# Two filler tiles that shift every SBUF buffer of the left side by 160 bytes

## The chip, the cores and the metric

The kernel runs on one core of one Trainium2 chip. The metric is the device time of one execution in microseconds (us), told as the median of several runs. Before the change it is 2169.11 us, the median of 3 runs between 2166.14 and 2170.45 us.

## The reference

Two post-norm layers over 512 tokens of width 2048, all in float32:

```python
# layer 0: one projection feeds stick-breaking attention (8 heads x 128) and a pooling mixer
h = x @ w_in                                   # 2048 x 6144
q, k, v, g_a, u, g_b = split(h)
o_a = stick_breaking_attention(q, k, v)
o_b = multiscale_pool(u, w_pool, pool_scale)   # windows 2, 4, 8, 16
y = concat([o_a * silu(g_a), o_b * silu(g_b)]) @ w_out
x = layer_norm(alpha * x + y)
# layer 1: RWKV-7 time mixing, 32 heads x 64
xr, xw, xk, xv, xa, xg = token_shift_mixes(x, mu)
r, k, v, g = xr @ w_r, xk @ w_k, xv @ w_v, xg @ w_g      # four 2048 x 2048 products
w, a = lora(xw), lora(xa)
o = wkv7_scan(r, decay(w), k, v, kk, a)        # state of 64 x 64 a head, 512 steps
y = ((group_norm(o) + bonus) * silu(g)) @ w_o
x = layer_norm(alpha * x + y)
```

## The kernel before

Every large float32 product is made of three products of a shorter format (fp32r): both operands are split into a high part and the rest (`split`, L133: ScalarE copies the high part, VectorE or GpSimd subtracts it), and TensorE adds high x high, high x low and low x high into the same PSUM bank (`mm3`, L138 to L142; `mm3b`, L484 to L488). A matmul has a moving operand, here mostly 512 columns that stream through the array, and a stationary one of 128 columns, the weights of the array, which a separate load (PEld) brings in while the matmul before it still streams. Both are read from the SBUF.

The core goes through these stages, in the order of time (us from the start of the span):

- 0 to 611: layer 0's input projection (`gemm_a`, L156): moving operand is the transposed input `x0_k` (tile `x` in the profile), stationary are the split weights `whi` and `wlo`. Between its groups of 24 matmuls small pieces of the attention are issued (`pump`, L45, L175); the gate columns from about 380 us on have almost none.
- 611 to 800: layer 0's output projection and layer norm (`proj_ln`, L421): here the weights `whi` and `wlo` move, 512 columns (three blocks) or 256 (two), and the gated rows `mixed` are stationary; the sums are called `gb`.
- 810 to 1430: layer 1's projections for k, r and g, again `gemm_a`: moving is the shifted input `mx`, stationary `whi` and `wlo`. k and r have side jobs between the groups (`ssq`, `low`, `loa`, `prew`, `prea`, `pb`), g has none after its first column block. In the first column block of each the tiles `mx` are still being made (`mixes`).
- 1430 to 1940: the RWKV recurrence in chunks (`scan`, L812), small float32 products with waits on each other, and between them the fourth projection v (`vps`, `vproj`, L842), whose weights come from another pool, `swp`.
- 1940 to 2168: output projection of layer 1 (`y`, `gb`) and the last layer norm. `proj_ln` is called without its first column block here, which the end of the scan has done as `y`. The next block (c0 = 512) still takes its weights from `swp`, the ones after it from the pool `wp1` (L1210, `start`, L1213).

Each engine runs its instructions in program order. The order is set by the code and, in the scan, by planned slots; the change touches neither.

What the change touches is where tiles lie. The pools of the SBUF are stacked from two sides: from the left upwards (`cst`, `wp`, `x0`, `att`, `set`, `stmp`, `res1`, `wp1` and others), and from the right downwards those opened with `side="right"` (`cst1`, `mix0` with `mixed`, `mx`, `swp`, `ld`). A pool's place follows from the sizes of what was opened before it on its side. Each tile of 128 partitions takes its bytes at the same address in every partition.

The product, the weights' tiles and the loop that reads them:

```python
149        self.nc.sync.dma_start(raw, ap)
151        hi = pool.tile([P, ww], F32R, tag="whi", name="whi", **kw)[:, :a * b]...
152        lo = pool.tile([P, ww], F32R, tag="wlo", name="wlo", **kw)[:, :a * b]...
...
172                for n in range(2):
173                    self.mm3(ps[n], hi[:, kk, n * P:(n + 1) * P], lo[:, kk, n * P:(n + 1) * P],
174                             xs[k][:, 0, :], xs[k][:, 1, :], k == 0, k == kblocks - 1)
```

One block of 128 weights is 512 bytes of a partition and one moving operand is 2048, so within one stage all moving operands start at one address modulo 512 and all weights at one.

Of the kernel before, what the change touches and what calls it, by code (L numbers as in the profile page):

```python
# [8 lines left out]
F32 = mybir.dt.float32  # L9
# [8 lines left out]
P = 128  # L18
# [16 lines left out]
class Kernel:  # L35
# [17 lines left out]
    def setup(self):  # L53
        nc, tc, ctx = self.nc, self.tc, self.ctx
        self.cst = ctx.enter_context(tc.tile_pool(name="cst", bufs=1))
        self.dram = ctx.enter_context(tc.tile_pool(name="dram", bufs=1, space=DRAM))
        self.lctx = ctx.enter_context(ExitStack())
        self.open_pools()
        c = self.cst
        ident = self.ident = c.tile([P, P], F32, name="ident")  # L60
        make_identity(nc, ident)
        self.eps = {}
        for e in (LN_EPS, GN_EPS):
            t = self.eps[e] = c.tile([P, 1], F32, name=f"eps{len(self.eps)}")
            nc.gpsimd.memset(t, e)
# [1140 lines left out]
    def layer1_out(self, x1_d, mixed, y_d):  # L1206
        nc, tc, i = self.nc, self.tc, self.i
        with ExitStack() as ctx:
            rp = ctx.enter_context(tc.tile_pool(name="res1", bufs=6))
            wp = ctx.enter_context(tc.tile_pool(name="wp1", bufs=2))  # L1210
            bv = {}

            def start(c0):  # L1213

                if c0 == 1024:
                    self.wp, self.ww = wp, 1024
                    for n, ap in (("g1", i["ln_g"][1:2]), ("b1", i["ln_b"][1:2])):
                        t = bv[n] = rp.tile([P, D], F32, name="ln" + n, bufs=1)
                        nc.sync.dma_start(t, ap.to_broadcast([P, D]))

            def residual(t, c0, w):
                r = rp.tile([P, 512], F32, tag="xr", name="xr")[:, :w]
                nc.sync.dma_start(r, x1_d[t * P:(t + 1) * P, c0:c0 + w])
                return r

            def after(t, sf, mean, rstd):
                g, b = bv["g1"], bv["b1"]
                out = lambda sl: nc.sync.dma_start(self.out[0, t * P:(t + 1) * P, sl], sf[:, sl])
                rstd = rstd()
                cut = 1792 if t == NT - 1 else 1024  # L1230
                dve = [slice(c, min(c + 512, cut)) for c in range(0, cut, 512)]
                rest = [slice(c, min(c + 512, D)) for c in range(cut, D, 512)]
                for sl in dve:
                    nc.vector.scalar_tensor_tensor(sf[:, sl], sf[:, sl], mean, g[:, sl], ALU.subtract, ALU.mult)
                nmr = rp.tile([P, 1], F32, tag="nmr", name="nmr", bufs=2)
                nc.vector.scalar_tensor_tensor(nmr, mean, -1.0, rstd, ALU.mult, ALU.mult)
                for sl in rest:
                    nc.scalar.activation(sf[:, sl], sf[:, sl], AF.Identity, scale=rstd, bias=nmr)
                    nc.gpsimd.tensor_mul(sf[:, sl], sf[:, sl], g[:, sl])
                    nc.gpsimd.tensor_add(sf[:, sl], sf[:, sl], b[:, sl])  # L1240
                for sl in dve:
                    nc.vector.scalar_tensor_tensor(sf[:, sl], sf[:, sl], rstd, b[:, sl], ALU.mult, ALU.add)
                    out(sl)
                for sl in rest:
                    out(sl)
                yield

            def first(t):
                y = rp.tile([P, 512], F32, tag="y", name="y", bufs=2)
                nc.sync.dma_start(y, y_d[t])  # L1250
                return y

            self.proj_ln(ctx, i["od_w_o"][0], mixed, residual, after, first, start)
# [29 lines left out]
```

## Time and profile before

| | |
|---|---|
| median of 3 runs | 2169.11 us |
| the profiled execution | 2169.39 us, its span 2167.7 us |
| mean granted TensorE clock | 0.988 of full speed |
| PE (matmul) busy | 2107.6 us, 97% |
| PEld (weight load) busy | 1690.7 us, 78% |
| DVE / ACT / POOL busy | 1274.2 / 952.1 / 265.1 us |
| 128x512 matmuls of layer 0's input projection | 2304, mean 389 to 392 ns |
| 128x512 matmuls of layer 1's k, r and g | 2304, mean 398 to 399 ns |

A matmul's duration in these rows runs from its start until its last column has been written, and the next one starts long before that. What a stream of them costs is the distance from start to start: a stretch in which nothing else runs, divided by the count of matmuls in it.

### The profile page before, as it was taken

To read this page: it belongs to the slowest core of one execution; us is meant where nothing else is said; L and a number is where in the kernel's file an instruction comes from. 1 tells how busy PE (TensorE), PEld (TensorE's weight loads), DVE (VectorE), ACT (ScalarE), POOL (GpSimd) and SP (SyncE) were. 2 spreads that over 40 slices of the span, in tenths; PEclk is the share of its full clock that TensorE was granted. 3 is DMA by queue.
4 is the path that set the end of the run, shared out by engine and by line. 5 is a ranking of instruction groups with operands and counts; after the bars stand their busy time and mean duration, and the time that the engine had idled before them with its cause. 6 is when DMAs were issued, how large, how long until landed. Compare 5 with 4: busy or idle time off the path is not lost. (4 is left out here: it accounts for less than half of the span.)

```text
span 2167.7 us, 33268 instructions
## 1 busy us (share of the span) xinstructions
PE 2107.6 (97%) x12915; PEld 1690.7 (78%) x12915; DVE 1274.2 (59%) x2557; ACT 952.1 (44%) x1663; POOL 265.1 (12%) x333
## 2 busy tenths in 40 slices
PE   8999999999999989998999989999999999999997
PEld 7888888888887887776788768867777777767786
DVE  4334335454433368677777872276787877876336
ACT  3335445332321258455555652254555555554211
POOL 0000000000000000233000020022333333310003
PEclk9999999999999999999999999998999999999998
DMA  5322222323233453554466663321232332332633
GB/s 188 97 73 83 79 73 68 98 93 102 94 106 116 132 175 113 159 169 143 161 221 215 215 234 131 107 68 55 89 99 74 100 102 69 104 111 95 228 103 112
DMA packets 214029, 262.94 MB, mean 121 GB/s; under 512 B 15768, under 2 KB 161776, under 8 KB 213104
## 3 DMA queue, kind: packets, MB, share of 16 engines
q1 hardware_dynamic: 213872, 260.83, 37.4%
q8 instruction: 101, 1.65, 0.3%
q14 instruction: 56, 0.46, 0.1%
HBM read 214.32 MB, written 46.47 MB: 120 GB/s over the span
## 5 line engine op out<-in xcount | busy, mean ns | idle before, releaser
L136 DVE TENSOR_TENSOR wlo<-wraw,whi 128x1024 fp32r<-128x1024 f32 (+1 forms) x268 | 314.1, 1175 | 501.4 <-ACT whi L135 487.1
L135 ACT CAST whi<-wraw 128x1024 fp32r<-128x1024 f32 (+1 forms) x324 | 303.4, 938 | 651.4 <-PE ga L141 319.0
L140 PE MATMUL ga<-mx,whi 128*128 128x512 f32 x768 | 305.4, 398 | 6.0 <-ACT mx L135 6.0
L141 PE MATMUL ga<-mx,whi 128*128 128x512 f32 x768 | 306.5, 399 | 3.8 <-DVE mx L136 3.8
L142 PE MATMUL ga<-mx,wlo 128*128 128x512 f32 x768 | 305.6, 398 | 0.0
L140 PE MATMUL ga<-x,whi 128*128 128x512 f32 x768 | 300.9, 392 | 0.0
L142 PE MATMUL ga<-x,wlo 128*128 128x512 f32 x768 | 299.5, 390 | 0.5 <-DVE wlo L136 0.5
L141 PE MATMUL ga<-x,whi 128*128 128x512 f32 x768 | 299.1, 389 | 0.0
L486 PE MATMUL gb<-whi,mixed 128*128 128x512 f32 (+1 forms) x576 | 198.6, 345 | 1.6 <-DVE s L437 1.6
L488 PE MATMUL gb<-wlo,mixed 128*128 128x512 f32 (+1 forms) x576 | 197.5, 344 | 2.4 <-DVE wlo L136 2.4
L487 PE MATMUL gb<-whi,mixed 128*128 128x512 f32 (+1 forms) x576 | 198.3, 344 | 0.0
L140 PEld LDWEIGHTS ga<-mx,whi 128*128 128x128 f32 x768 | 145.5, 189 | 43.7 <-ACT mx L135 7.4
L141 PEld LDWEIGHTS ga<-mx,whi 128*128 128x128 f32 x768 | 145.4, 189 | 41.7 <-DVE mx L136 6.8
L142 PEld LDWEIGHTS ga<-mx,wlo 128*128 128x128 f32 x768 | 145.5, 189 | 35.3 <-issue 0.3
L142 PEld LDWEIGHTS ga<-x,wlo 128*128 128x128 f32 x768 | 144.2, 188 | 31.4 <-DVE wlo L136 0.9
L140 PEld LDWEIGHTS ga<-x,whi 128*128 128x128 f32 x768 | 144.3, 188 | 29.4 <-ACT whi L135 0.3
L141 PEld LDWEIGHTS ga<-x,whi 128*128 128x128 f32 x768 | 144.3, 188 | 29.1
L140 PE MATMUL vps<-mx,whi 128*128 128x512 f32 x256 | 122.0, 476 | 0.3 <-ACT vT L858 0.3
L488 PEld LDWEIGHTS gb<-wlo,mixed 128*128 128x128 f32 x576 | 108.2, 188 | 17.6 <-DVE wlo L136 3.2
L486 PEld LDWEIGHTS gb<-whi,mixed 128*128 128x128 f32 x576 | 108.2, 188 | 17.4 <-DVE s L437 2.9
L487 PEld LDWEIGHTS gb<-whi,mixed 128*128 128x128 f32 x576 | 108.5, 188 | 13.7
L136 POOL TENSOR_TENSOR wlo<-wraw,whi 128x512 fp32r<-128x512 f32 x56 | 73.8, 1318 | 244.6 <-ACT whi L135 194.8
(331 smaller groups left out, 3508.1 us busy)
## 6 DMA issues: line engine op xcount, KB each, us to landing
wraw<-in_ev_w_in SPq DMA_DIRECT2D x96, 512.0 KB, 3.5
wraw<-in_ev_w_out SPq DMA_DIRECT2D x32, 512.0 KB, 3.6
wraw<-in_od_w_k SPq DMA_DIRECT2D x32, 512.0 KB, 4.5
wraw<-in_od_w_r SPq DMA_DIRECT2D x32, 512.0 KB, 4.4
wraw<-in_od_w_g SPq DMA_DIRECT2D x32, 512.0 KB, 3.5
wraw<-in_od_w_v SPq DMA_DIRECT2D x64, 256.0 KB, 2.8
ar_d<-pAR SPq DMA_DIRECT2D x16, 512.0 KB, 2.6
bk_d<-pBK SPq DMA_DIRECT2D x16, 512.0 KB, 3.3
```

Source lines behind the costliest of these rows:

```text
L135: self.nc.scalar.copy(hi, src)
L136: (eng or self.nc.vector).tensor_sub(lo, src, hi.bitcast(F32))
L140: mm(ps, ah, bh, start=start, stop=False)
L141: mm(ps, ah, bl, start=False, stop=False)
L142: mm(ps, al, bh, start=False, stop=stop)
L486: mm(ps, ah, bh, start=start, stop=False)
L487: mm(ps, al, bh, start=False, stop=False)
L488: mm(ps, ah, bl, start=False, stop=stop)
```

## The change

Two tiles are allocated that nothing reads or writes. The first, 40 x 4 = 160 bytes a partition, is the first tile of the first pool of the left side, so that every tile on the left lies 160 bytes higher. The second, 112 x 4 = 448 bytes, is the first tile of the pool `res1`, and shifts only what is allocated after it in the output of layer 1.

```diff
@@ setup
         c = self.cst
+
+        c.tile([P, 40], F32, name="pad0")
         ident = self.ident = c.tile([P, P], F32, name="ident")
@@ layer1_out
             rp = ctx.enter_context(tc.tile_pool(name="res1", bufs=6))
+            rp.tile([P, 112], F32, name="pad1", bufs=1)
             wp = ctx.enter_context(tc.tile_pool(name="wp1", bufs=2))
```

The sequence of instructions of every engine, their operands' shapes and their waits are the same in both programs; only addresses differ. The start addresses of the operands modulo 512, as the two programs allocate them:

| matmuls | count | moving, before | weights, before | moving, after | weights, after |
|---|---|---|---|---|---|
| layer 0 input, `ga<-x` | 2304 | 288 | 288 | 448 | 448 |
| layer 0 output, `gb`, 512 columns | 576 | 288 | 448 | 448 | 448 |
| layer 0 output, `gb`, 256 columns | 384 | 288 | 448 | 448 | 448 |
| layer 1 k, r, g, `ga<-mx` | 2304 | 448 | 288 | 448 | 448 |
| layer 1 v, `vps` | 768 | 448 | 448 | 448 | 448 |
| layer 1 output, `y` (by tile) | 132 / 60 | 288 / 448 | 448 | 448 | 448 |
| layer 1 output, `gb`, c0 = 512 | 192 | 448 | 448 | 448 | 448 |
| layer 1 output, `gb`, c0 = 1024 | 192 | 352 | 448 | 448 | 448 |
| layer 1 output, `gb`, 256 columns | 384 | 352 | 448 | 448 | 448 |
| scan, `xo<-M,AR` | 112 | 288 | 448 | 448 | 448 |
| scan, other products with both operands on one side | | equal shift | equal shift | | |

## Rows read from the trace of the kernel before

**Rows 1.** The page, busy time of TensorE (share of the span, instructions).
```profile
PE 2107.6 (97%) x12915; PEld 1690.7 (78%) x12915; DVE 1274.2 (59%) x2557; ACT 952.1 (44%) x1663; POOL 265.1 (12%) x333
```

**Rows 2.** The page's costliest groups: count, busy us, mean ns, idle before.
```profile
L141 PE MATMUL ga<-mx,whi 128*128 128x512 f32 x768 | 306.5, 399 | 3.8 <-DVE mx L136 3.8
...
L141 PE MATMUL ga<-x,whi 128*128 128x512 f32 x768 | 299.1, 389 | 0.0
```

**Rows 3.** PE alone by stretch: from:to, us, busy (count), granted clock, DMA share, GB/s.
```profile
535.00:600.00 65.00, 65.00 (x289) 1.00 0.31 98
1310.00:1380.00 70.00, 70.00 (x301) 1.00 0.38 121
2041.00:2059.00 18.00, 18.00 (x81) 1.00 0.75 260
2070.00:2100.00 30.00, 30.00 (x130) 1.00 0.32 104
620.00:655.00 35.00, 35.00 (x152) 1.00 0.26 90
2110.00:2150.00 40.00, 40.00 (x340) 1.00 0.29 99
```

**Rows 4.** PE groups between 2040 and 2059 us, weights from the pool swp.
```profile
L486 PE MATMUL gb<-whi,mixed 128*128 128x512 f32 x29 | 11.3, 389 | 0.0
```

**Rows 5.** PE groups between 2063 and 2100 us, weights from the pool wp1.
```profile
L486 PE MATMUL gb<-whi,mixed 128*128 128x512 f32 x52 | 20.6, 396 | 0.0
```

**Rows 6.** PE groups between 834 and 1020 us, the k stage.
```profile
L141 PE MATMUL ga<-mx,whi 128*128 128x512 f32 x224 | 88.8, 396 | 0.0
```

**Rows 7.** Tile ga between 30 and 360 us: ns min/median/max, first and last start.
```profile
L141 PE MATMUL ga<-x,whi x404: 387/389/475, 29.7 to 359.9; 128*128 128x512 f32 x135
```

**Rows 8.** PE in order of time after an interruption: start us, us, what.
```profile
521.27 0.40 PE L141 MATMUL ga<-x,whi 128*128 128x512 f32 x1
521.50 0.39 PE L142 MATMUL ga<-x,wlo 128*128 128x512 f32 x1
521.73 0.40 PE L140 MATMUL ga<-x,whi 128*128 128x512 f32 x1
521.97 0.39 PE L141 MATMUL ga<-x,whi 128*128 128x512 f32 x1
522.20 0.39 PE L142 MATMUL ga<-x,wlo 128*128 128x512 f32 x1
522.42 0.39 PE L140 MATMUL ga<-x,whi 128*128 128x512 f32 x1
```

**Rows 9.** What PE waited for between 800 and 1440 us: total us, times, longest.
```profile
PE ssq L646 <- ACT sqr L135: 6.5, 1, 6.5
PE ga L140 <- ACT mx L135: 6.0, 3, 3.9
PE ga L141 <- DVE mx L136: 3.8, 4, 1.7
```

**Rows 10.** PE groups between 613 and 748 us, output projection of layer 0.
```profile
L486 PE MATMUL gb<-whi,mixed 128*128 128x512 f32 x189 | 75.1, 397 | 1.6 <-DVE s L437 1.6
L487 PE MATMUL gb<-whi,mixed 128*128 128x512 f32 x189 | 75.0, 397 | 0.0
L488 PE MATMUL gb<-wlo,mixed 128*128 128x512 f32 x189 | 73.9, 393 | 0.0
```

**Rows 11.** PE groups by shape over the whole span: 256 columns and the scan.
```profile
L486 PE MATMUL gb<-whi,mixed 128*128 128x256 f32 x256 | 72.1, 283 | 0.0
...
L1000 PE MATMUL xo<-M,AR 128*128 128x128 f32 x224 | 49.6, 304 | 2.1 <-DVE M L1026 1.2 <-DVE M L1024 0.7
...
L487 PE MATMUL y<-wo,mixed 128*128 128x512 f32 x64 | 25.5, 399 | 0.0
...
L142 PE MATMUL po<-wh,v 128*128 128x256 f32 x8 | 2.3, 282 | 0.0
```

**Rows 12.** All engines by stretch: from:to, us, PE, PEld, DVE, ACT, POOL, clock, DMA.
```profile
400.00:600.00 200.00, 199.81 (x880) 164.57 (x879) 91.38 (x116) 62.59 (x80) 0.56 (x5) 1.00 0.31 98
800.00:1000.00 200.00, 193.31 (x835) 150.63 (x834) 140.25 (x175) 120.57 (x200) 48.02 (x47) 0.99 0.49 149
1000.00:1200.00 200.00, 193.48 (x818) 154.71 (x817) 150.19 (x211) 113.96 (x180) 13.96 (x30) 0.98 0.56 188
```

## The prediction before the run

> **What bounds the kernel now.** I read the page first, then its costliest groups, then single stretches of the matmul engine, and last the waits. PE is busy for 97% of the span [rows 1], so the question is what a matmul costs in a stream, not who waits for whom. The groups hold the first hint: the 2304 matmuls of layer 1's k, r and g (three rows like the one shown, 398 to 399 ns) last 7 to 9 ns longer than the 2304 of layer 0's input projection (389 to 392 ns) [rows 2]. Both come from the same function, with the same shape.
>
> Durations overlap, so I take the distance from start to start. In a stretch that holds nothing but one kind of matmul it is (length + 0.39 us) / count, since the count includes the matmul that is cut at the edge. Layer 0's gates: 65.39/289 = 226.3 ns. Layer 1's g: 70.40/301 = 233.9 ns. Both stretches have the full clock and no idle time [rows 3]. So 7.6 ns, 3.2%, go somewhere.
>
> Is it the address? The trace has a test of its own in the output projection of layer 1, where the same loop first takes weights from `swp` and then from `wp1`. With both operands at 448 modulo 512 it runs at 18.39/81 = 227.0 ns, and from about 2062 us on, with 352 against 448, at 30.40/130 = 233.8 ns [rows 3]; the mean duration goes from 389 to 396 ns [rows 4, 5]. Engine, line, shape and stationary tiles are the same on both sides. The fast stretch is even the one with more DMA traffic (260 against 104 GB/s), so contention with transfers doesn't explain it. In every stage I read, equal residues go with 226 to 227 ns in a steady stream and unequal ones with 233 to 234 (differences of 160 and 416), or 35.39/152 = 232.8 (difference 352, layer 0's output) [rows 3]. The fast level is seen at 288/288 and at 448/448, so it is the difference that counts, not the place.
>
> **The change part by part.** It adds, removes and moves no instruction. The filler tiles cost no time: nothing writes them. The left side moves by 160 bytes, from 288 to 448, and meets the right side's 448.
>
> *k, r and g.* 2304 matmuls go from unequal to equal: 2304 x 7.6 ns = 17.5 us. Two deductions. First, an aligned stream isn't fast at once after another job: behind an interruption the starts lie 0.23, 0.23, 0.24, 0.23 and 0.22 us apart and then settle at 0.226 [rows 8], 1.15 us for five against 5 x 0.226 = 1.13, so 20 to 25 ns lost each time. k and r have 2 x 32 groups of 24 matmuls, nearly all with a job behind them: 64 x 25 ns = 1.6 us. The misaligned stream has nothing to lose there: 396 ns in k with its side jobs [rows 6], as in g's pure stretch. That an interrupted stage still gains is seen in the attention stage, where the median is 389 ns although small jobs break in [rows 7]. Second, the first column block of each stage is fed by tiles still in the making (waits of 6.0 and 3.8 us on ACT and DVE [rows 9]); 3 x 96 matmuls can gain 2.2 us there, and I give half of it, 1.1, to longer waits. The 6.5 us wait for `sqr` stays. That leaves 17.5 - 1.6 - 1.1 = 14.8 us; bounds: 12 (the whole first blocks lost and twice the loss at the breaks) and 17.5.
>
> *Output of layer 0, 512 columns.* 576 matmuls. The three lines have 397, 397 and 393 ns against 389 when aligned [rows 10, 4]: 6.7 ns on average; from starts, 232.8 - 227.0 = 5.8 [rows 3]. I take 6.2: 3.6 us, bounds 3.3 and 3.9.
>
> *Output of layer 1, c0 = 1024.* 192 x (233.8 - 227.0) = 1.3 us.
>
> *The 256-column blocks.* 768 matmuls. The trace has no long aligned stream of 256 columns. Nearest rows: short aligned ones in the attention last 282 ns, against 283 for `gb` [rows 11], which says 0 to 1 ns; but those are all within reach of an interruption. Half of the loss of a 512-column stream would be 3.5 ns. Bounds 0 and 2.7 us; I take 1.0, nearer to the rows.
>
> *Scan and `y`.* Of the `y` matmuls 132 become equal, in bursts of three, where even aligned ones hardly reach the fast level (`y`, a mix of both, has 399 ns [rows 11]): 0.3 us. The 112 products `xo<-M,AR` (224 rows of 304 ns [rows 11]) become equal as well. `vps` was aligned before, and products with both operands on the left keep their difference. I take 0 for the scan, with 1.5 us either way: 3% of the 49.6 us of that group.
>
> *Other engines.* VectorE, ScalarE and the transfers get other addresses too. I cost this at nothing: between 400 and 1200 us PE covers them, busy for 193 to 200 of each 200 us while DVE has at most 150 and ACT 121 [rows 12].
>
> Sum: 14.8 + 3.6 + 1.3 + 1.0 + 0.3 = 21.0 us. From the profiled execution's own 2169.4 us (span 2167.7 and 1.7 around it) that makes 2148.4; the median of the runs shown is 2169.1, only 0.3 below, so the forecast is 2148 us.
>
> A rule of the Trainium skill speaks against all this: it ("TensorE: Matmul & The Clock Gate", section "Step-by-step: what each phase is for") says that TensorE has two independent read ports of the SBUF, one for the moving operand and one for the weight load, and that loading the next weights takes no bandwidth from the running matmul. By it the residue of the one against the other could not matter, and the change would give 0. The trace disagrees: 227.0 and 233.8 ns in one loop [rows 3]. The ports may be two; the rows say that what lies behind them is not indifferent to the address.
>
> **The rivals.**
>
> *Only quiet stages gain.* In k and r the side work on DVE and ACT may set the pace once PE is faster, because `prep`, the squares and the mixes share those engines with the splitting of weights. For it: DVE is busy for 140 to 150 of 200 us there, against 91 in the gates, and the waits on `mx` and `sqr` lie in these stages [rows 9, 12]. Against: outside the first column blocks PE shows no idle time in k [rows 6], and 3% less time raises DVE's share only from 0.75 to 0.77. Then k and r give nothing: 768 x 7.6 = 5.8 (g) + 3.6 + 1.3 + 1.0 = 11.7 us, so 2157.7 us.
>
> *Nothing changes.* What I took for the address is something else that differs between the stages, such as the tiles' absolute place or which pool the weights come from. For it: `swp` and `wp1` are two pools, not one pool moved. Against: two boundaries in the trace, near 611 and near 2062 us, follow the residues, with different tiles on both. Time: 2169 us. The rule on independent read ports, told above, would come to this.
>
> *Slower: the level belongs to weights at 288.* All long fast stretches of layer 0 have their weights at 288, that is 32 modulo 64, and the change takes them to 448, that is 0. Were that residue the cause, layer 0's input projection would fall to the slow level, 2304 x 7.6 = 17.5 us, and layer 1 would gain nothing: 2169.4 + 17.5 = 2187 us. It is slower from the point where layer 0's loss exceeds what of the 21 us is left. Against: the stretch from 2041 to 2059 us is fast with both operands at 448 [rows 3].
>
> **How the numbers follow.** Forecast 0.84, quiet stages alone 0.08, nothing 0.04, slower 0.04. The forecast's own range comes from its bounds: gains of 12 + 3.3 + 1.3 + 0 - 1.5 = 15 to 17.5 + 3.9 + 1.3 + 2.7 + 1.5 = 27 us, both ends unlikely together; 2143 to 2154. To hold 8 in 10 with the first rival half in, I give 2143 to 2156. A measurement of this kernel tells 0.2%, 4.3 us, from no change. Faster by more: the first two cases, 0.92. Within: 0.04. Slower: 0.04.
>
> **What would show it.** Right: the `ga<-mx` groups fall from 396 ns to about 389 in steady stretches, and their starts to 226 or 227 ns apart; `gb` in layer 0 to about 389; layer 0's input projection ends at the same time as before, near 611 us; the stage of g is shorter by some 5 us. The waits on `mx` and `sqr` stay or grow by up to 1 us. Wrong: `ga<-x` above 389 ns (the absolute place matters), `ga<-mx` at 389 with new idle time in front of it (supply bounds), or `ga<-mx` still at 396 (not the address). A scan that is longer or shorter by more than 2 us would say that the small products depend on addresses too, and break the sum.

## The result and the profile after

| | median, us | range | runs |
|---|---|---|---|
| before | 2168.39 | 2164.88 to 2170.95 | 6 |
| after | 2153.43 | 2151.27 to 2158.38 | 6 |

The ratio is 0.994, with a 95% interval from 0.9927 to 0.9953: a gain of 10 to 16 us, where 21 were forecast. The time lies inside the range, but the forecast's own 2148 lies outside the interval of the measurement; the first rival, 2157.7, is nearer: 4.3 us from the median, against 5.4.

The profiled execution of after took 2158.4 us (span 2156.7), some 5 us above its median. Single stages below are therefore shown from two traces of the same program, this one and its repetition (the first experiment), before a difference of a microsecond is believed.

First the pace, the thing the change aims at. This is PE alone by stretch in the kernel after (from:to, us, busy and count, granted clock, DMA share, GB/s):

```profile
535.00:600.00 65.00, 65.00 (x288) 1.00 0.31 98
1310.00:1380.00 70.00, 70.00 (x311) 1.00 0.38 121
620.00:655.00 35.00, 35.00 (x156) 1.00 0.27 91
2060.00:2090.00 30.00, 30.00 (x135) 1.00 0.32 103
2100.00:2140.00 40.00, 40.00 (x335) 1.00 0.29 97
```

They answer to [rows 3]. With the prediction's formula: layer 0's gates 65.39/288 = 227.0 ns (226.3 before); g 70.40/311 = 226.4 (233.9); layer 0's output 35.39/156 = 226.9 (232.8); layer 1's output at c0 = 1024 30.39/135 = 225.1 (233.8). All four 512-column streams now run at one level (one matmul more or less in the count is 1.7 ns in a window of 30 us and 0.8 ns in one of 65). The last line has 256 columns, where a matmul lasts 0.28 us: 40.28/335 = 120.2 ns against 40.28/340 = 118.5 before. That one became slower.

The page's groups and busy times say the same, and answer to [rows 1] and [rows 2] (count, busy us, mean ns, idle before):

```profile
PE 2087.6 (97%) x12915; PEld 1688.5 (78%) x12915; DVE 1272.0 (59%) x2557; ACT 951.8 (44%) x1663; POOL 266.1 (12%) x333
...
L143 PE MATMUL ga<-mx,whi 128*128 128x512 f32 x768 | 302.0, 393 | 3.8 <-DVE mx L138 3.8
...
L143 PE MATMUL ga<-x,whi 128*128 128x512 f32 x768 | 299.3, 390 | 0.0
```

`ga<-mx` fell from 399 to 393 ns, `ga<-x` stayed. PE is still busy for 97%: a share of busy time doesn't show such a gain.

But a faster stream is not yet a shorter stage. The lengths of the stages, from the start of the first matmul of one to that of the next, the last one to the end of its last matmul (us), in three traces:

| stage | before | after | after, repeated | forecast change |
|---|---|---|---|---|
| layer 0 up to its gates | 344.9 | 344.7 | 344.8 | 0 |
| layer 0's gates | 257.4 | 257.4 | 257.4 | 0 |
| layer 0's output, 512 columns | 136.6 | 132.6 | 132.7 | -3.6 |
| layer 0's output, 256 columns, and up to k | 60.1 | 62.0 | 63.3 | about -0.5 |
| k, r, g: first column blocks, together | 91.7 | 92.6 | 90.2 | -1.1 |
| k, the rest | 186.1 | 183.6 | 182.4 | k, r, g: |
| r, the rest | 183.2 | 184.0 | 183.9 | -13.7 |
| g, the rest | 159.3 | 154.5 | 154.5 | together |
| scan, from the first `vps` to the first `y` | 506.9 | 501.4 | 501.2 | 0 |
| `y` | 76.6 | 76.3 | 77.0 | -0.3 |
| layer 1's output, c0 = 512 | 46.6 | 50.3 | 47.2 | 0 |
| layer 1's output, c0 = 1024 | 45.0 | 43.5 | 43.6 | -1.3 |
| layer 1's output, 256 columns | 45.7 | 46.2 | 46.2 | about -0.5 |

Layer 0's output, g and c0 = 1024 gained what their pace says. r gained nothing, though behind its first block it has the same 672 matmuls as g, which gained 4.8 us. The scan's 5.5 us and the 50.3 come from something else (below).

What r ran into instead shows in what PE waited for between 1054 and 1238 us in the kernel after (total us, times, longest us):

```profile
PE pb L809 <- DVE rkr L138: 2.1, 4, 0.7
PE prew L144 <- DVE w2h L138: 1.3, 1, 1.3
PE pb L809 <- ACT rkr L137: 0.2, 1, 0.2
```

The same window of the kernel before has one line:

```profile
PE pb L807 <- DVE rkr L136: 0.2, 1, 0.2
```

3.4 us of new waits, on results of DVE in `prep`. DVE isn't full there, so what did it wait for itself? Its waits between 1054 and 1235 us, after:

```profile
DVE pn L792 <- DMA pk<-k_d: 28.2, 10, 5.2
DVE pn L792 <- DMA pn<-rn_d: 8.2, 3, 3.7
```

and before:

```profile
DVE pn L790 <- DMA pk<-k_d: 27.8, 10, 3.4
...
DVE pn L790 <- DMA pn<-rn_d: 5.1, 2, 3.5
```

So DVE stood still for some 33 us in r already before, in front of one product that needs a load. One of these stops in the kernel after, DVE in order of time (start us, us, what, idle before and its releaser):

```profile
1201.05 0.74 DVE L803 SCALAR_TENSOR_TENSOR pr<-pr,vec,pk 128x512 f32<-128x512 f32 x1
1201.71 1.22 DVE L138 TENSOR_TENSOR wlo<-wraw,whi 128x1024 fp32r<-128x1024 f32 x1
1202.84 0.69 DVE L138 TENSOR_TENSOR rkr<-pr,rkr 128x512 fp32r<-128x512 f32 x1
1206.80 0.75 DVE L792 SCALAR_TENSOR_TENSOR pn<-pk,hkk,pn 128x512 f32<-128x512 f32 x1 [3.27 <-DMA pk<-k_d]
1207.46 1.22 DVE L138 TENSOR_TENSOR wlo<-wraw,whi 128x1024 fp32r<-128x1024 f32 x1
```

and SP's queue around it (start us, us, what):

```profile
1201.16 0.36 SPq L801 DMA_DIRECT2D bk_d<-pBK  x1
1201.64 0.35 SPq L812 DMA_DIRECT2D bc_d<-pbc  x1
1202.09 0.81 SPq L764 DMA_DIRECT2D pk<-k_d  x1
```

The load of the next `pk` is issued at 1202.09; `pn`, which needs it, already stands at the head of DVE's queue at 1203.5. All that is behind it on DVE, splits of weights and of `rkr` among it, stands with it until 1206.8. The Trainium skill ("TensorE: Matmul & The Clock Gate", section "Step-by-step: what each phase is for") says that PE is the only engine that reorders its instructions; these rows agree: `wlo` follows `pn` without a gap, though ACT had finished its half of that split at 1203.40:

```profile
1202.36 1.04 ACT L137 CAST whi<-wraw 128x1024 fp32r<-128x1024 f32 x1
```

In the kernel before, PE's own slowness covered these stops. That is a theory from waits; the second and third experiments test it.

### The profile page after: what moved, and what is told of

It is laid out like the page before. It is cut to its first block, busy times and chain, and to the rows that moved or that the text cites. A ratio compares the mean times of both kernels' runs of the same rounds, so it can differ in the third digit from the quotient of the medians.

```text
span 2156.7 us, 33268 instructions
## 1 busy us (share of the span) xinstructions
PE 2087.6 (97%) x12915; PEld 1688.5 (78%) x12915; DVE 1272.0 (59%) x2557; ACT 951.8 (44%) x1663; POOL 266.1 (12%) x333
## 4 chain that ended last, share of the span: by engine, by line
PE 82%; DVE 9%; DMA 4%; ACT 2%; issue 1%; POOL 1%; SPq 0%; DVEq 0%; ACTq 0%
PE ga L142 14%; PE ga L144 13%; PE ga L143 13%; PE gb L488 4%; PE gb L490 4%; PE gb L489 4%; PE vps L142 4%; PE vps L143 2%; PE vps L144 2%; PE xo L1004 2%; PE sa L1010 2%; PE g L877 2%; PE xo L1002 2%; DVE wlo L138 1%; PE xo L1030 1%
## 5 line engine op out<-in xcount | busy, mean ns | idle before, releaser
L142 PE MATMUL ga<-mx,whi 128*128 128x512 f32 x768 | 301.3, 393 | 5.6 <-ACT mx L137 5.6
L143 PE MATMUL ga<-mx,whi 128*128 128x512 f32 x768 | 302.0, 393 | 3.8 <-DVE mx L138 3.8
```

The lines of the kernel that those rows point to most:

```text
L142: mm(ps, ah, bh, start=start, stop=False)
L143: mm(ps, ah, bl, start=False, stop=False)
```

## The experiments

Two questions are open. Why did r give nothing: because DVE stands still in front of `pn` (my theory), or because the load on DVE and ACT sets r's pace, whatever the order (the rival)? And does the difference between two addresses set the level of a stream (my theory), or the place of one of them (the rival)? The expectations are quoted as they were written ahead of each run.

**The change again**, the same program:

> The changed kernel once more, beside the experiments on the same chip, for a second trace. Theory A (the residue modulo 512 sets a matmul's pace, and part of the gain is lost to new waits): 2153 us within 4, ga<-mx at 227 to 228 ns from start to start, and again no gain in r behind its first column block (183 to 185 us long), because PE waits there for rkr and w2h. Rival B (what r lost was a chance of one execution): r is 177 to 179 us long in this trace.

2154.98 us (2153.70 to 2155.63), ratio 0.9938 [0.9925, 0.9951]. Its stages stand in the table above. r is again without gain; c0 = 512 is not again longer, so the 50.3 belongs to one execution: there PE waited 4.3 us for `wlo`, against 2.4 before, and ran 3.4 us at a granted clock of 0.50.

**After, with `pn` issued behind the pair's scan on DVE.** The product is the same; it is told to stand later in DVE's queue:

```diff
-        nc.vector.tensor_tensor_scan(L, ...)
+        sc = nc.vector.tensor_tensor_scan(L, ...)
...
-        nc.vector.scalar_tensor_tensor(rn, k, col(self.hv["kk"]), rn, ALU.mult, ALU.mult)
+        with self.tc.issue_after(sc.ins):
+            nc.vector.scalar_tensor_tensor(rn, k, col(self.hv["kk"]), rn, ALU.mult, ALU.mult)
```

> The changed kernel with one instruction moved: on DVE's queue the product rn = k * k_k * rn of the next pair stands behind that pair's scan, no longer ahead of the rest of the chain of the pair before it, so that DVE doesn't stand still for the load of pk. Theory A (r lost its gain because DVE, the supplier of rkr and w2h, stood still 28 + 8 us for loads at the head of its queue): these waits all but vanish, PE's waits in r (some 5 us) too, r behind its first block falls from 184 to 178 to 179 us, and the time is 4 to 6 us under the changed kernel's. Rival B (DVE's work itself is too long for a PE that is 3% faster): r stays at 183 to 185 us and the time is that of the changed kernel.

2145.11 us (2141.21 to 2149.56), ratio 0.9887 [0.9866, 0.9907]. That is 8 to 10 us under the kernel after and its repetition, where 4 to 6 were expected. In r behind its first block PE waits for nothing any more, and DVE's longest waits between 1054 and 1235 us are for ACT's half of the split and for `ptw` (total us, times, longest):

```profile
DVE wlo L138 <- ACT whi L137: 26.6, 17, 4.3
DVE pL L783 <- ACT ptw L781: 8.8, 13, 2.0
```

The lines on `pk` and `pn` are gone; DVE's stops in this window come to 36 us, against 46 in the kernel after, and they now stand ahead of what DVE is early for. r behind its first block takes 178.4 us instead of 184.0. Not foreseen: g's first block falls from 34.6 to 28.0 us as well.

**Before, with the same edit.** By my theory r has nothing to gain from it while PE is slow:

> The same move of one DVE instruction in the kernel before. Theory A: before, PE waited only 0.6 us for rkr in r, so there is at most 1 us to win: 2167 to 2169 us, r behind its first block 182 to 184 us. Rival (the standstill on DVE costs by itself, whatever the addresses): 4 to 6 us faster here as well, 2163 us.

2157.83 us (2156.19 to 2162.91), ratio 0.9957 [0.9941, 0.9973]. The expectation for r held and that for the whole missed by far: 10 us faster. The rival, that the standstill costs by itself, came nearer, though not in r. The four traces, r behind its first block and g's first block:

| us | unequal residues | equal residues |
|---|---|---|
| `pn` early: r / g's first block | 183.2 / 34.6 | 184.0 / 34.6 |
| `pn` late: r / g's first block | 182.8 / 27.3 | 178.4 / 28.0 |

r needs both edits: in these traces either alone gives next to nothing, both give 4.8 us. By the rival r could not come to 178.4 with the same work on DVE and ACT. Over all thirteen traces of this document r takes 183.2 to 186.0 us with `pn` early and `ga<-mx` at the slow pace (four traces), 181.9 to 186.5 with `pn` early and the fast pace (five), 182.8 with `pn` late and the slow pace (one) and 178.4 with `pn` late and the fast pace (three). Where the time goes is seen by column block of 96 matmuls (us, the second to the eighth of r):

| kernel | 2 | 3 | 4 | 5 | 6 | 7 | 8 |
|---|---|---|---|---|---|---|---|
| before | 25.69 | 26.17 | 26.17 | 26.17 | 26.17 | 26.17 | 26.62 |
| after | 25.05 | 25.55 | 25.55 | 25.61 | 26.09 | 26.46 | 29.64 |
| after, repeated | 25.33 | 25.55 | 25.55 | 25.55 | 25.55 | 26.03 | 30.35 |
| before, `pn` late | 25.73 | 26.17 | 26.17 | 26.17 | 26.17 | 26.17 | 26.17 |
| after, `pn` late | 25.13 | 25.55 | 25.55 | 25.55 | 25.55 | 25.55 | 25.55 |

So r did gain from the addresses, 0.6 us a block, and gave it back at its end, most of it in the last block, in which DVE also makes the first tiles `mx` for g. The slow stream doesn't always cover the stop: with the left side shifted by 32 and by 128 bytes (below; `ga<-mx` at 232 to 234 ns) PE waits 2.1 and 1.7 us for `w2h` in the last block, runs 3.4 us at a granted clock of 0.50 after that, and the block takes 29.97 and 29.77 us.

The edit did more than move `pn`: the program was ordered anew around it. From r's fourth block to the seventh the order on DVE differs by `pn` alone, and that on PE, ACT and SP not at all; what blocks 6 and 7 lost is thus shown to come from that one stop. At r's start, at the end of its last block and in g's first block other instructions of these engines change places as well, so that what is shown there is the worth of the new order, not of the one stop. g's first block needs only the second edit, in both kernels. What PE waited for there, between 1238 and 1275 us, in this experiment (in the kernel before DVE's `mx` has 3.8 us there, the whole of its line in [rows 9], and ACT's 2.2):

```profile
PE ga L141 <- DVE mx L136: 0.4, 1, 0.4
```

**Layer 0 misaligned, all else as before**, by 160 bytes ahead of x alone:

```diff
+        xp.tile([P, 40], F32, name="padx")
         xs = [...]
```

> The kernel before with a filler of 160 bytes ahead of the tiles x0 alone: layer 0's moving operands lie at 448 modulo 512, its weights stay at 288; all else is as before. Theory A (the difference counts): ga<-x goes from 227 to 234 ns from start to start and from 389 to 396 ns of duration, layer 0's input projection ends 15 to 16 us later, 2183 to 2185 us in all. Rival (weights at 288 are fast whatever moves): no change, 2168 us. Rival (two independent read ports, no effect of any address): no change as well.

2182.26 us (2181.47 to 2183.10), ratio 1.0064 [1.0049, 1.0079]: 14 us slower. PE between 545 and 610 us:

```profile
545.00:610.00 65.00, 65.00 (x279) 1.00 0.29 90
```

65.39/279 = 234.4 ns where [rows 3] have 226.3. The two stages of layer 0's input grew by 8.2 and 6.8 us. 2304 x 7.6 = 17.5 would have been the full price. A column block of 96 matmuls pays it, 0.73 us, where no job breaks in; those of the attention grew by 0.60 to 0.66 us. That fits the prediction's deduction, by which only an aligned stream loses at an interruption.

**The right side moved to meet the left, at 288:**

```diff
+        cp.tile([P, 40], F32, name="padr")
         mixed, mix_ctx = self.layer0(cp)
...
+            rp.tile([P, 112], F32, name="pad1", bufs=1)
```

> The other way to bring both sides together: the kernel before with the filler of 160 bytes on the right side, which moves that side's tiles down from 448 to 288 modulo 512, and the filler of 448 bytes in res1; the left side stays where it was. Theory A (only the difference counts): the time of the changed kernel, 2153 us within 4, with ga<-mx at 227 ns. Rival (the new place of the left side's tiles, 448, made it faster, for any engine): no change, 2168 us.

2155.05 us (2153.68 to 2161.35), ratio 0.9953 [0.9936, 0.9971]. PE in layer 0's gates and in g:

```profile
535.00:600.00 65.00, 65.00 (x289) 1.00 0.31 98
1310.00:1380.00 70.00, 70.00 (x311) 1.00 0.37 121
```

65.39/289 = 226.3 and 70.40/311 = 226.4 ns with all operands at 288, as with all at 448: the difference counts, not the place. The rival of the place is out.

**Other shifts of the left side**, by 32, 128 and 416 bytes instead of 160 and without the second filler; one time each, for the pace alone:

```diff
+        c.tile([P, 8], F32, name="pad0")      # or [P, 32], or [P, 104]
```

> The kernel before with a filler of 32 bytes on the left: weights at 320, so that moving and weights differ by 128 (k, r, g), 384 (output of layer 0) and 448 (output of layer 1, second block on). Theory A in its strict form (only equal residues are fast): 231 to 235 ns from start to start in all three, 2165 to 2171 us. Rival (any difference that is a multiple of 128 is fast, since the unit is smaller than 512): 227 ns in k, r, g, and some 2155 us.

> The kernel before with a filler of 128 bytes on the left: weights at 416, differences of 32 (k, r, g), 480 (output of layer 0) and 32 the other way (output of layer 1, second block on). Theory A in its strict form: 231 to 235 ns, 2165 to 2171 us. Rival (near is good enough, the loss grows with the distance): between 227 and 230 ns and some 2157 us.

> The kernel before with a filler of 416 bytes on the left: weights at 192, differences of 256 (k, r, g; output of layer 0) and 192 (output of layer 1, second block on). Theory A in its strict form: 231 to 235 ns, 2165 to 2171 us. Rival (the unit is 256 bytes): 227 ns in k, r, g and in layer 0's output, some 2154 us. Rival (half of 512 is the worst place): above 236 ns and over 2172 us.

2161.28, 2167.67 and 2157.69 us, beside 2166.84 for the kernel before; the first and the third lie between the times expected by theory and rival. PE between 1310 and 1380 us, by 32:

```profile
1310.00:1380.00 70.00, 70.00 (x303) 1.00 0.37 121
```

by 128:

```profile
1310.00:1380.00 70.00, 70.00 (x301) 1.00 0.35 113
```

by 416:

```profile
1310.00:1380.00 70.00, 70.00 (x310) 1.00 0.37 118
```

That is 70.40/303 = 232.3, 233.9 and 227.1 ns, at differences of 128, 32 and 256 bytes between moving operand and weights. 256 is as good as 0: "modulo 512" in the change's description, and in my prediction, is twice too strict.

**The second experiment with a second filler of 128 bytes**, which should suit 256 columns and hurt 512:

```diff
-            rp.tile([P, 112], F32, name="pad1", bufs=1)
+            rp.tile([P, 32], F32, name="pad1", bufs=1)
```

> The changed kernel with the DVE instruction moved, as before, and the second filler cut from 448 to 128 bytes, so that in the output of layer 1 from the block c0 = 1024 on the moving weights lie at 128 against 448 (192 apart, modulo 256). Theory A2 (from the earlier traces: equal modulo 256 is fastest for 512 columns, but slowest for 256 columns, where 448 modulo 512 gave 113.4 ns against 120.3): the 512-column block goes from 227 to 233 ns, 192 x 6 = 1.2 us longer, the 256-column blocks from 120.3 to 113 to 114 ns, 384 x 6.9 = 2.6 us shorter, so the last stretch of 256 columns is 2 to 2.6 us shorter; in all 1.4 us under the same kernel with 448 bytes, about 2144 us, hardly to be told in the time. Rival (the 113.4 ns came from another cause in that one run): 256 columns stay at 119 to 121 ns and the time rises by 1 us.

2146.84 us (2140.79 to 2148.87), ratio 0.9895 [0.9879, 0.9911]: no difference from the second experiment that the time can tell. The paces can be told apart. PE in layer 1's output, 256 columns and then 512:

```profile
2085.00:2115.00 30.00, 30.00 (x267) 1.00 0.26 88
2040.00:2070.00 30.00, 30.00 (x131) 1.00 0.26 88
```

30.28/267 = 113.4 ns against 120.2 with equal residues, and 30.39/131 = 232.0 against 225.1. The stages move by -2.5 us (46.2 to 43.7) and +1.2 us (43.6 to 44.8).

**The change without its second filler:**

> The change without its second filler: everything as in the changed kernel but the output of layer 1 from c0 = 1024 on, whose weights lie at 0 against 448 (64 apart). Theory A2: 192 matmuls of 512 columns at 229 instead of 227 ns, 0.4 us longer, 384 of 256 columns at 117.5 to 118 instead of 120.3, 1.0 us shorter; the same time as the changed kernel within 1 us, 2153 to 2155 us, so the second filler brings nothing. Rival (theory A as predicted, with 233.8 ns for every unequal residue and 256 columns no slower when equal): 1.3 to 2.3 us slower than the changed kernel.

2153.66 us (2152.88 to 2160.37), ratio 0.9931 [0.9911, 0.9952]: the same as with it. c0 = 1024 then runs at a difference of 64 bytes, in 44.0 us instead of 43.5, and the 256 columns take 45.4 instead of 46.2; 28.28/240 = 117.8 ns:

```profile
2100.00:2128.00 28.00, 28.00 (x240) 1.00 0.23 79
```

What the filler gains in one block it loses in the other.

**The second experiment with a second buffer for `l1r`.** There k had given back about half of what r gained (186.2 us behind its first block, against 183.6 after), and ACT waited for one load between 850 and 1015 us (9.5 us in the kernel after):

```profile
ACT l1h L137 <- DMA l1r<-in_od_a: 9.7, 2, 6.3
```

```diff
-            wr = kp.tile([P, 3, 96], F32, tag="l1r", name="l1r")[:, :nk]
+            wr = kp.tile([P, 3, 96], F32, tag="l1r", name="l1r", bufs=2)[:, :nk]
```

> The changed kernel with the DVE instruction moved, and a second buffer for the raw LoRA weights l1r of the k stage. Theory A (k lost a third of its gain in the same way as r, ACT standing still 9.7 us at the head of its queue for the load of l1r, and PE then 1 to 2 us for the squares): ACT's wait for l1r mostly goes, PE has no wait for sqr inside k, and k behind its first block is 181 to 182 us instead of 182.4 to 186. Rival (the loads come too late whatever the buffers, or the squares wait for something else): k stays at 182 to 186 us.

2141.12 us (2139.64 to 2145.45), ratio 0.9870 [0.9851, 0.9889], the fastest of all: 1.3%, some 28 us, below the kernel before. The line on `l1r` is gone, k takes 182.4 us. What k had lost can be told. In the second experiment PE waited between 833 and 1015 us:

```profile
PE ssq L648 <- DVE sqr L138: 2.1, 1, 2.1
```

and right behind that wait its clock fell to the lower of its two levels, 1.2 GHz (PE alone, from:to, us, busy and count, granted clock, DMA share, GB/s):

```profile
923.00:927.40 4.40, 2.27 (x11) 1.00 0.07 24
927.40:930.80 3.40, 3.40 (x9) 0.50 0.63 201
```

Half of 3.4 us is lost by that: 182.4 + 2.1 + 1.7 = 186.2. The second experiment with the filler of 128 bytes has 186.6 us, a wait of 2.5 us and the same fall; the kernel after a wait of 1.1 us, no fall, and 183.6. It is not settled that the second buffer removes the wait: the repetition of after has neither wait nor buffer, and 182.4 us, and the interval of the whole time overlaps with that of the second experiment.

## Why the prediction was partly right

**Right: the mechanism.** The level depends on the difference between the operands' addresses (four 512-column streams to 225 to 227 ns, `ga<-x` untouched; undone by the misaligned layer 0; got again at another place). The rivals "nothing changes" and "weights at 288" are out: 288/288 and 448/448 run alike. The rule of the Trainium skill weighed in the prediction, that moving operand and weight load have read ports of their own and don't disturb each other ("TensorE: Matmul & The Clock Gate", section "Step-by-step: what each phase is for"), doesn't hold in these traces: 227 or 234 ns at the same instructions, by the addresses of the two.

**Right: layer 0's output and c0 = 1024.** Forecast 3.6 and 1.3 us, measured 4.0 and 1.4 (3.9 and 1.4 in the repetition).

**Wrong: the term of 14.8 us for k, r and g.** Measured: 5.7 us in one trace (620.3 to 614.6) and 9.3 in the other (611.0), below the lower bound of 12. g's 4.8 came in full; k gave 2.5 to 3.6; r nothing; the first column blocks nothing that two traces agree on. The wait for `sqr` in r's first block, 6.5 us, which the prediction let stand, grew to 7.6 and 7.3. Even with `pn` late in both kernels the term is 8.2 us (611.3 to 603.1), and 11.4 with the second buffer. The step that failed is the argument that stages with side jobs keep their gain, less the loss at the breaks and in the first blocks, since PE shows no idle time there. That was seen for k, from [rows 6]; r was taken along. The loss at the breaks was sized well: a block of r without stops gained 0.62 us, where g's gained 0.73. And I judged DVE's spare time by its busy share, 0.75 [rows 12], which says nothing about an engine that stands with its queue behind one load: those stops were in the trace of before, 33 us of them, and I had read the waits of PE only.

**Half right: the rival of quiet stages.** Its result for r holds, not that for k, and its time is nearer than mine. Its cause does not hold: with the same work on DVE and ACT in another order, r gains in full.

**Wrong in sign, and small: the 256 columns.** Forecast a gain of 1.0 us; in layer 1 the pace fell back from 118.5 to 120.2 ns, 0.5 us lost. I had carried a rule over from 512 columns and given it half of its price. In layer 0 the pace is the same in both, about 120 ns; what that stage lost in the table lies at its edges: waits on `s` of 1.7 and 2.1 us, of which the kernel before has its 1.6 in the stage ahead [rows 10], and 2.2 and 1.7 us lost near its end at a granted clock of 0.50.

**The scan: a test of mine that misled.** I had written that a scan off by more than 2 us would show small products to depend on addresses. It is 5.5 us shorter, but the third experiment, with the addresses of before, has 501.7 us, and the second, with the addresses of after, 506.8. The difference is the clock. In the two long scans, from 48.5 us behind their start, PE runs 13.7 us at the lower level of the clock (all engines, busy of PE, PEld, DVE, ACT, POOL, then granted clock, DMA share, GB/s), in the kernel before:

```profile
1463.00:1478.00 15.00, 14.25 (x194) 10.55 (x192) 12.63 (x42) 7.19 (x17) 3.87 (x3) 1.00 0.32 96
1479.10:1492.80 13.70, 13.70 (x89) 9.94 (x88) 5.37 (x16) 2.69 (x9) 2.89 (x4) 0.50 0.01 2
```

in the second experiment:

```profile
1459.90:1473.60 13.70, 13.70 (x94) 10.17 (x95) 5.38 (x18) 2.53 (x8) 2.90 (x4) 0.50 0.01 2
```

and the same place of the third, without it:

```profile
1471.30:1485.00 13.70, 13.45 (x166) 10.06 (x168) 10.15 (x34) 5.00 (x14) 4.18 (x5) 1.00 0.13 41
```

PE is busy for as long and gets 89 or 94 against 166 matmuls done. So long a stretch at this place is in these two of the thirteen traces alone, one with the addresses of before and one with those of after. Ahead of it PE was nearly always busy, 14.25 of 15 us at full clock; why the clock fell in these executions stays open.

**Luck in the total.** The time lies inside the range although the largest term fell below its bound. The two traces of after are 11.0 and 15.7 us shorter than that of before, and 5.5 and 5.7 us of this are the scan, which the clock made longer with either set of addresses; 5.5 and 10 us are left for the change, with what it set off. How many of the executions without a trace have such a scan isn't known, and so not how much of the 15.0 us between the medians is the change.

## What to carry to other kernels

Compare the start-to-start distance of equal matmuls across stages: where it differs by 3% at the same shape, clock and no idle time, look at the operands' addresses. Before a gain per instruction is multiplied by their number, look in each stage at what the engines that feed it stand still for, not at how busy they are: a stop that the slower stream covers can become the next bound. A hoisted instruction that needs a late load blocks everything behind it on its engine; moving that one instruction, with what changed places around it, brought 10 us to the kernel before and 8 to 10 to the kernel after.

## What the runs showed of the hardware

The pace by the difference of start addresses, moving operand less weights, modulo 256 bytes; ns from start to start within one stream at full clock, over all thirteen traces (from the start times, which tell more than a count in a short window):

| difference | 0 | 32 | 64 | 96 | 128 | 160 | 192 | 224 |
|---|---|---|---|---|---|---|---|---|
| 512 columns | 227 | 233.4 | 229 | 233.5 | 232.7 | 234.2 | 233.3 | 233.5 |
| 256 columns | 120.0 | 116.7 | 117.8 | 120.0 to 120.3 | 118.8 to 119.7 | 117.3 to 118.7 | 113.4 | 118.3 |

For 512 columns one value, 0, is best and 64 is next; 0 was met both as 0 and as 256. For 256 columns the best is 192, and 0 is among the worst, so no single shift suits both shapes. The 117.3 and the 118.7 at 160 come from kernels with the very same addresses in that stage, so that for 256 columns something else counts too, by as much as 1.4 ns. All of it is for fp32 data in the format fp32r and 128x128 weights that change with each matmul; why the two shapes differ, and what in the memory makes the difference of addresses count, the runs don't say.
